# A decoder layer with 32 experts: contiguous rows in the gather, row splits between the transposes, gate loads on another queue

## The chip, the cores and the metric

The kernel runs on one core of a Trainium2 chip. A core has a matrix engine (TensorE, PE in the profile), a vector engine (VectorE, DVE), a scalar engine (ScalarE, ACT), GpSimd (POOL) and SyncE (SP), which here only issues transfers. Each engine works through its own list of instructions in order and waits on semaphores for the others. Sixteen DMA engines move data between the device memory and SBUF, the on-chip memory of 128 partitions; TensorE writes to PSUM, a small memory of banks of 512 float32 per partition.

The metric is the device time of one execution in microseconds (us). A profile is the record of one such execution.

## The reference

One layer on 256 tokens of 2048 features, all in float32. The mixers (a convolution, a gated linear attention, a windowed attention, a short convolution), the output projection and the first layer norm come first and are the same in both kernels. What the change touches comes after:

```python
x = layer_norm(DN_ALPHA * x + mix @ w_out[i], ln1_g[i], ln1_b[i])
ffn = hier_moe(x, ...)                       # 32 experts, two per token
ple = sigmoid(x @ ple_w_gate[i] + ple_b_gate[i]) * (p[i] @ ple_w_proj[i])
x = layer_norm(DN_ALPHA * x + ffn + ple, ln2_g[i], ln2_b[i])
```

In `hier_moe` each token picks one of four groups of experts by one softmax, then the two best of the eight experts in that group. An expert is `(silu(t @ w_gate) * (t @ w_up)) @ w_down` with 256 inner features, weighted by the router's gate. The weights of one expert are 6 MiB, so the 32 experts hold 192 MiB, and all but those of experts without tokens have to be read.

## The kernel before, in words

**Before the router.** The input projections, the mixers and the output projection take the first 408 us. Products run in a split form: a float32 matrix is cast to the faster format `fp32r` (high part), the rest is a second `fp32r` matrix (low part), and the products of the parts are added.

**The router stage** (L749 to L961). The rows are normalized without scale and bias (`xn`, tokens on the partitions). TensorE transposes them, two blocks of 128 features per step of the loop at L783, and the evictions from PSUM apply scale and bias, one block on DVE (L796), one on ACT (L793): that gives `x1T`, features on the partitions. The router's logits follow by matmuls (`route`). After the loop, `xn` is split for the gather: ACT casts four pieces of 1024 columns to `xnh` (L809), POOL subtracts four times to get `xnl` (L810). Then comes a chain of small DVE operations (L836 to L912): maxima, one-hot masks, counts, the order of the experts by their number of tokens, and a place (a "seat") for each token and expert. SP reads the order of the experts into registers before it issues the experts' weight loads.

**The gather** (L929). Ten groups have 128 seats each, in four units of 32; a unit belongs to one expert. `selection` builds a 0/1 matrix `M` (tokens by seats of two groups, 256 columns), and the gather is a matmul of rows of `xnh` and `xnl` with `M`, four per block of 128 features: 64 for all 16 blocks. Feature d = 16 p + k goes to partition p of block k, because the experts' weights lie in the device memory with 16 rows of a matrix behind each other on one partition; the 128 columns of `xn` that form the stationary operand of one matmul are therefore 16 elements apart (`k0 + j::KT`). The evictions apply scale and bias (`g16`, `b16`) on DVE and ACT. The first gather serves groups 0 and 1: half of it ahead of group 0, the rest between its first steps. The odd groups 1, 3, 5 and 7 carry the next gather between their own steps.

**The groups** (`experts`, L1027). For each group: `gu` matmuls of the gathered rows with gate and up weights in steps (8 steps when the group has four experts, 4 when it has two), each step reading one of five 2 MiB slots of SBUF; then silu and product on ACT and DVE, a transposition (`hT`), the down product in four steps of 512 columns (`y`), each followed by a scatter of the previous step (`sc`, the transposed selection matrix), which DVE adds into the result rows. Groups 0, 1, 2, 4, 8, 9 have four experts, groups 3, 5, 6, 7 two. In group 9 the loads of experts without tokens are skipped.

**The gate.** `ple` needs x1 @ ple_w_gate, a matmul of 256 x 2048 x 2048. It is cut into pieces (`layer_input_gate`, L720): for four column blocks db, 16 pieces of one feature block each, two token halves per piece; the end of a column block adds the product with `ple_w_proj`. The pieces fill TensorE between the steps of the groups: `pump(rate)` is called after each `gu` step, and `fill` after the silu, after `hT` and after each `y` step, which in the odd groups first takes the steps of the gather. `RT[g]` (L1143) says how many pieces a call gives. Eight short tasks that start the sum come before the pieces (`start_sum`), eight that spread the rows of the last norm behind. Two pieces and then one are issued in the router stage. Gate weights come in loads of 0.5 MiB for two pieces, into six buffers; the weights of pieces 9 to 32 (`in_slots`, pairs 4 to 15) lie instead in three of the five expert slots, which come free after pieces 16, 24 and 32.

**What sets the order.** TensorE's instructions in the groups, and those of TensorE, DVE and ACT in the router stage, stay in the order in which they are written; the other engines are ordered by a planner. SP issues all weight loads, those of the experts and of the gate, in one order, and waits at each for its buffer to be free.

Of the kernel before, what the change touches and what calls it, by code (L numbers as in the profile page):

```python
# [19 lines left out]
P = 128  # L20
# [69 lines left out]
def _layout(inp):  # L90

    lasting, early = _shape_tables()
    by_k = lambda w: w.reshape(KT, P, -1).transpose(1, 0, 2).reshape(P, -1)
    vec = lambda a: np.asarray(a).reshape(-1, P).T
    gla = Columns()
    for name in ("conf_dw_w", "conf_dw_b"):
        early.add(name, vec(inp[name]))
    for name in ("conf_ln_g", "conf_ln_b", "mix_scale", "gla_b_g2", "gla_norm_g",
                 "sc_conv_w", "ln1_g", "ln1_b"):
        lasting.add(name, vec(inp[name]))  # L100
    lasting.add("g16", np.asarray(inp["ln1_g"]).reshape(P, KT))
    lasting.add("b16", np.asarray(inp["ln1_b"]).reshape(P, KT))
    lasting.add("rbias", np.tile(np.concatenate([inp["router_g_b"][0], inp["router_e_b"][0]]), (P, 1)))
    vecs = np.zeros((2, 32, 512), np.float32)
    vecs[:, :20] = np.concatenate([np.asarray(inp[n]).reshape(4, 512) for n in
                                   ("ple_b_gate", "ln1_g", "ln1_b", "ln2_g", "ln2_b")])
    lasting.add("wr", by_k(np.concatenate([inp["router_g_w"][0], inp["router_e_w"][0]], axis=1)))
    w_in = np.asarray(inp["w_in"])[0]
    gla.add("wgl", by_k(np.pad(w_in[:, 2048:2064], ((0, 0), (0, 16)))))
    gla.add("wg2", np.tile(np.pad(inp["gla_w_g2"][0], ((0, 16), (0, 0))), (4, 1)))  # L110
    gla.add("relb", inp["rel_bias"])
    tiles = lambda w: w.reshape(2, 8, P, 512).transpose(0, 2, 1, 3)
    by_cols = lambda w: np.stack([tiles(w[:, c:c + 512]) for c in range(0, D, 512)])
    return {
        "vecs": vecs.reshape(64, 512), "lasting": lasting.array(), "early": early.array(), "gla": gla.array(),
        "xT": np.asarray(inp["x"])[0].T.reshape(KT, P, T).transpose(1, 0, 2),
        "x": inp["x"], "pT": np.asarray(inp["p"])[0, 0].T.reshape(2, P, T).transpose(1, 0, 2),
        "w_in": np.stack([tiles(w_in[:, c:c + 512]) for c in BLOCKS.values()]),
        "w_out": by_cols(np.asarray(inp["w_out"])[0]), "ple_w_gate": by_cols(np.asarray(inp["ple_w_gate"])[0]),
        "exp_w_gu": np.concatenate([inp["exp_w_gate"][0], inp["exp_w_up"][0]], axis=2),  # L120
        "exp_w_down": np.asarray(inp["exp_w_down"])[0], "ple_w_proj": np.asarray(inp["ple_w_proj"])[0],
    }, (lasting.at, early.at, gla.at)

# [2 lines left out]
def trunk(ctx, tc, where, vecs_d, lasting, early, gla, xT, x, pT_d, w_in, w_out, ple_w_gate, exp_w_gu, exp_w_down, ple_w_proj, out):  # L126
# [28 lines left out]
    def f32(ap):  # L155
        return ap.bitcast(F32)
# [544 lines left out]
    small = [(db, i) for db in range(4) for i in (*range(8 * db, 8 * db + 8), 32 + db) if i not in in_slots]  # L701
    ple_w = {}

    def ple_load(n=1):
        for _ in range(min(n, len(small))):
            db, i = small.pop(0)
            w = work([P, 2, 512], name="plw")
            if i < 32:
                nc.sync.dma_start(w, ple_w_gate[db, (i // 4) % 2, :, 2 * (i % 4):2 * (i % 4) + 2])
            else:  # L710
                nc.sync.dma_start(w, ple_w_proj[:, db * 512:(db + 1) * 512].rearrange("(k p) c -> p k c", p=P))
            ple_w[i] = w


# [32 lines left out]
    tasks.append(layer_input_gate())  # L747

    x1T = bm.tile([P, KT, T], F32, name="x1T", tag="ma")  # L749
    ple_load(6)  # L750
    for i in in_slots[::4]:
        s = load_half(ple_w_gate[i // 8, (i // 4) % 2], "plw")
        for j in range(4):
# [23 lines left out]
    def route(k2):  # L777
        for k in (2 * k2, 2 * k2 + 1):
            o = 64 * (k % 2)
            PE.matmul(rl[o:o + 36, 0:T], wr[:, k, :], x1T[:, k, :], start=k < 2, stop=k >= KT - 2,  # L780
                      skip_group_check=True, tile_position=(0, o))

    for k2 in range(KT // 2):  # L783
        b = bank("x1t", *tags[k2])
        for j in range(2):
            for t in range(NT):
                k = 2 * k2 + j
                PE.transpose(b[:, (j * NT + t) * P:(j * NT + t + 1) * P],
                             xs[t][k // 8][:, (k % 8) * P:(k % 8 + 1) * P], ident)
        for j in range(2):  # L790
            k = 2 * k2 + j
            if j:
                S.activation(x1T[:, k, :], b[:, j * T:(j + 1) * T], AF.Identity, scale=col("ln1_g", k),  # L793
                             bias=col("ln1_b", k))
            else:
                V.tensor_scalar(x1T[:, k, :], b[:, j * T:(j + 1) * T], col("ln1_g", k), col("ln1_b", k),  # L796
                                op0=ALU.mult, op1=ALU.add)
        if k2 > 2:
            route(k2 - 3)
    for k2 in range(KT // 2 - 3, KT // 2):  # L800
        route(k2)
    lt = stage([P, P], F32, name="lt", tag="mt", bufs=1)
    V.tensor_scalar(lt, const("io")[:, 0:P], const("sid")[:, 0:1], None, op0=ALU.is_gt)
    V.tensor_copy(rls[0:36, :], rl[0:36, 0:T])
    S.copy(rls[64:100, :], rl[64:100, 0:T])
    for hf in range(2):
        for t in range(NT):
            hs = slice(1024 * hf, 1024 * hf + 1024)
            S.copy(xnh[:, t, hs], xn[:, t, hs])  # L809
            G.tensor_sub(xnl[:, t, hs], xn[:, t, hs], f32(xnh[:, t, hs]))  # L810
    rl2 = bank("rl2")
    for t in range(NT):
        PE.matmul(rl2[:, 64 * t:64 * t + 36], rls[:, t * P:(t + 1) * P], both, start=t == 0, stop=True,
# [115 lines left out]
    def gather(m_, n, xg, tags=(("mx", 2),)):  # L929

        w = n * P
        per = 512 // w
        for k0 in range(0, KT, per):
            b = bank("xg", *tags[k0 // per % len(tags)])
            for j in range(per):
                o = b[:, j * w:(j + 1) * w]
                for t in range(NT):
                    for i, part in enumerate((xnh, xnl)):
                        PE.matmul(o, part[:, t, k0 + j::KT], m_[:, t, :], start=j + t + i == 0, stop=t + i == 2,  # L939
                                  skip_group_check=True)  # L940
            for j in range(per):
                k = k0 + j
                if j % 2:
                    S.activation(xg[:, k], b[:, j * w:(j + 1) * w], AF.Identity, scale=const("g16")[:, k:k + 1],  # L944
                                 bias=const("b16")[:, k:k + 1])
                else:
                    V.tensor_scalar(xg[:, k], b[:, j * w:(j + 1) * w], const("g16")[:, k:k + 1],  # L947
                                    const("b16")[:, k:k + 1], op0=ALU.mult, op1=ALU.add)
            yield

    def gathered(n):
# [75 lines left out]
    def experts(g, units, xg, xo, rate=0, last=False, ahead=None):  # L1027
# [20 lines left out]
        for k0 in range(0, KT, kn):  # L1048
            s = expert_slot("we", g)[:, 0:ne * kn * 512].rearrange("p (q k f) -> p q k f", q=ne, k=kn)
            for q in range(ne):  # L1050
                if k0 == 0:
                    es_.append(nc.sync.value_load(orders[0:1, ranks[q]:ranks[q] + 1], min_val=0, max_val=NE - 1))
                src = exp_w_gu[bass.ds(es_[q], 1)].rearrange("o (p k) f -> p (o k) f", p=P)
                nc.sync.dma_start(s[:, q], src[:, k0:k0 + kn, :], **need[q])

            if g == 0 and k0:
# [83 lines left out]
            pass  # L1140
        return xg

    RT = [1.6, 1.3, 2, 1.3, 0.6, 1, 0.6, 1.6]  # L1143
    RT += [0.5] * (NG - len(RT))
    tasks.insert(0, start_sum())
    tasks.append(second_norm_rows())
# [68 lines left out]
```

## Time and profile before

| | us |
|---|---|
| median of 3 runs | 1011.82 |
| lowest, highest | 1008.22, 1013.42 |
| profiled execution | 1012.47 |
| its span, first to last instruction | 1010.7 |
| first expert load issued by SP | 438.81 |
| first `gu` matmul of group 0 | 450.91 |
| last matmul | 988.66 |

A row of the time order gives the start, the length, the engine, the line, what is written and read, and the number of instructions merged in the row. Matmuls overlap: the length of one includes its way through the array, so what one costs is read from the start of the next. A row of the groups gives busy time and the mean of one in ns, then the idle time ahead of it and who ended it. A wait is put down to the engine that came last.

### The profile page before, as it was taken

The numbers are of one execution on the slowest core, as the hardware profiler recorded it, in microseconds if no ns is written. First come the engines' busy times: TensorE is split into PE (matmuls) and PEld (weight loads), VectorE is DVE, ScalarE is ACT, GpSimd is POOL, SyncE is SP. The second block draws the span as 40 slices with busy tenths as digits, with TensorE's granted clock in tenths as the row PEclk, the third lists the DMA queues.
The fourth block names the chain that finished last, engine by engine and source line by source line (L and its number), as shares of the span: only waits on it lengthen the run. The fifth ranks groups of instructions, "written<-read, shape, count | busy, mean of one in ns | idle before, by whom it ended". The sixth has DMA issues, their size and how long they took to land. (4 is left out here: it accounts for less than half of the span.)

```text
span 1010.7 us, 14886 instructions
## 1 busy us (share of the span) xinstructions
PE 937.8 (93%) x5542; PEld 580.7 (57%) x5542; DVE 454.1 (45%) x891; ACT 294.2 (29%) x529; POOL 147.9 (15%) x107
## 2 busy tenths in 40 slices
PE   8999998999999999869999999999998899998991
PEld 6896997978898789544333453333541263461220
DVE  6554648997758545665031141111431233340327
ACT  6631643444665445611010120100221021020002
POOL 2131335335323332310000000000000000000002
PEclk9999999999999999979999999999999999999996
DMA  9961364445345852048999999999489999989982
GB/s 336 418 235 73 124 222 135 164 161 183 152 163 193 323 201 85 19 171 335 363 327 409 395 404 408 391 415 342 170 309 388 417 418 368 411 330 398 362 312 86
DMA packets 76655, 280.90 MB, mean 278 GB/s; under 512 B 7000, under 2 KB 7264, under 8 KB 64544
## 3 DMA queue, kind: packets, MB, share of 16 engines
q1 hardware_dynamic: 76256, 278.82, 72.7%
q0 software_dynamic: 320, 1.06, 0.3%
q8 instruction: 45, 0.74, 0.3%
q14 instruction: 34, 0.28, 0.1%
HBM read 290.33 MB, written 2.11 MB: 289 GB/s over the span
## 5 line engine op out<-in xcount | busy, mean ns | idle before, releaser
L1060 PE MATMUL gu<-we,xg 128*32 128x512 f32 x1184 | 158.7, 600 | 7.8 <-DMA we<-in_exp_w_gu_dram 7.7
L730 PE MATMUL pl<-plw,x1T 128*128 128x512 f32 x256 | 120.9, 611 | 1.2 <-DMA plw<-in_ple_w_gate_dram 1.2
L1060 PEld LDWEIGHTS gu<-we,xg 128*32 128x32 f32 x1184 | 37.6, 110 | 111.6 <-issue 78.7
L1098 PE MATMUL y<-wd,hT 128*32 128x512 f32 x624 | 93.0, 599 | 8.3 <-DMA wd<-in_exp_w_down_dram 4.8
L1114 DVE TENSOR_TENSOR xn<-xn,sc 128x512 f32<-128x512 f32 x76 | 50.3, 683 | 106.3 <-PE sc L1112 106.3
L1180 POOL TENSOR_TENSOR xn<-xn,gbB 128x512 f32<-128x512 f32 x2 | 3.2, 1582 | 564.0 <-ACT xn L1179 564.0
L730 PEld LDWEIGHTS pl<-plw,x1T 128*128 128x128 f32 x256 | 46.7, 192 | 66.0 <-issue 62.7
L1080 DVE SCALAR_TENSOR_TENSOR h<-h,gw,gu 128x256 f32<-128x256 f32 x10 | 4.8, 480 | 173.9 <-ACT h L1079 173.9
L1079 ACT ACTIVATE h<-gu 128x256 f32<-128x256 f32 x10 | 3.8, 383 | 215.0 <-PE gu L1060 215.0
L939 PE MATMUL xg<-M,xnh 128*128 128x256 f32 x160 | 62.9, 393 | 2.7 <-DVE M L926 2.4
L483 DVE SCALAR_TENSOR_TENSOR ya<-hp,ce,ya 128x255 f32<-128x255 f32 (+29 forms) x120 | 63.9, 586 | 0.0
L939 PE MATMUL xg<-M,xnl 128*128 128x256 f32 x160 | 62.2, 389 | 0.0
L1102 ACT CAST yh<-y 128x512 fp32r<-128x512 f32 x40 | 23.4, 586 | 118.8 <-PE sc L1111 69.7
L939 PEld LDWEIGHTS xg<-M,xnh 128*128 128x128 f32 x160 | 50.1, 313 | 12.4 <-issue 4.5
L245 ACT CAST wh<-wow 128x512 fp32r<-128x512 f32 (+1 forms) x80 | 42.5, 535 | 44.4 <-PE wo L288 32.8
L1098 PEld LDWEIGHTS y<-wd,hT 128*32 128x32 f32 x624 | 19.2, 109 | 62.2 <-issue 28.8
L288 PE MATMUL wo<-wh,ml 128*128 128x512 f32 (+1 forms) x160 | 54.6, 350 | 0.0
L287 PE MATMUL wo<-wh,mh 128*128 128x512 f32 (+1 forms) x160 | 54.1, 348 | 0.0
L939 PEld LDWEIGHTS xg<-M,xnl 128*128 128x128 f32 x160 | 50.5, 315 | 0.1
L248 DVE TENSOR_TENSOR wl<-wow,wh 128x512 fp32r<-128x512 f32 (+1 forms) x53 | 31.8, 602 | 38.7 <-ACT wh L245 34.3
L1103 DVE TENSOR_TENSOR yl<-y,yh 128x512 fp32r<-128x512 f32 x40 | 27.4, 685 | 46.7 <-ACT yh L1102 46.1
L944 ACT ACTIVATE xg<-xg,cl 128x256 f32<-128x256 f32 x40 | 22.6, 564 | 85.2 <-DVE xg L947 85.2
(480 smaller groups left out, 1977.3 us busy)
## 6 DMA issues: line engine op xcount, KB each, us to landing
we<-in_exp_w_gu_dram SPq DMA_DIRECT2D x168, 512.0 KB, 7.4
wd<-in_exp_w_down_dram SPq DMA_DIRECT2D x92, 512.0 KB, 10.7
we<-in_exp_w_gu_dram SPq DMA_DIRECT2D x32, 1024.0 KB, 12.4
wow<-in_w_out_dram SPq DMA_DIRECT2D x16, 1024.0 KB, 7.2
wd<-in_exp_w_down_dram SPq DMA_DIRECT2D x16, 1024.0 KB, 10.2
wd<-in_exp_w_gu_dram SPq DMA_DIRECT2D x24, 512.0 KB, 5.5
plw<-in_ple_w_gate_dram SPq DMA_DIRECT2D x20, 512.0 KB, 10.3
plw<-in_ple_w_gate_dram SPq DMA_DIRECT2D x6, 1024.0 KB, 6.9
```

Source lines behind the costliest of these rows:

```text
L245: S.copy(wh, w)
L248: e.tensor_sub(wl, w, f32(wh))
L287: PE.matmul(o, lh[:, k, ts], wh, start=i == 0, stop=False)
L288: PE.matmul(o, ll(k)[:, ts], wh, start=False, stop=False)
L483: V.scalar_tensor_tensor(ya[:, cb, d:T], hp[:, cb, 0:T - d], dww(30 - d, cb), ya[:, cb, d:T], op0=ALU.mult, op1=ALU.add)
L730: PE.matmul(bs[t], x1T[:, k, t * P:(t + 1) * P], s, start=False, stop=k == KT - 1, skip_group_check=True)
L939: PE.matmul(o, part[:, t, k0 + j::KT], m_[:, t, :], start=j + t + i == 0, stop=t + i == 2, skip_group_check=True)
L1060: PE.matmul(gu[us, :], xg[:, k0 + k, xo + us.start:xo + us.stop], s[:, q, k, :], start=k0 + k == 0, stop=k0 + k == KT - 1, skip_group_chec ...
L1098: PE.matmul(y[us, :], hT[:, k, us], s[:, q, k, c0:c0 + 512], start=k == 0, stop=k == 1, skip_group_check=True, tile_position=(0, us.start))
L1102: S.copy(yh, y)
L1103: V.tensor_sub(yl, y, f32(yh))
L1114: V.tensor_add(rows(acc, t, db), rows(acc, t, db), o)
```

## The change

Five things change.

- The experts' gate and up weights are laid out so that feature d = 128 k + p is on partition p of block k. The gather reads 128 neighbouring columns of `xnh` and `xnl` for each matmul, and its evictions use the columns of scale and bias that the transposes use. `g16` and `b16` go.
- The split of `xn` moves from behind the transposes to between them: in step k2 ACT casts one piece of 512 columns, and DVE (no longer POOL) subtracts the piece of the step before. Eight casts and eight subtractions instead of four and four.
- The gate's loads, but for the first six, are issued by GpSimd instead of SP.
- `RT` changes: fewer gate pieces in groups 0 and 2, more in group 1, none in group 3, the last ones in group 4.
- The view of `exp_w_gu` in the load follows the new layout.

```diff
@@ _layout
-    lasting.add("g16", np.asarray(inp["ln1_g"]).reshape(P, KT))
-    lasting.add("b16", np.asarray(inp["ln1_b"]).reshape(P, KT))
...
-        "exp_w_gu": np.concatenate([inp["exp_w_gate"][0], inp["exp_w_up"][0]], axis=2),
+        "exp_w_gu": np.concatenate([inp["exp_w_gate"][0], inp["exp_w_up"][0]], axis=2)
+        .reshape(NE, KT, P, 2 * DE).transpose(0, 2, 1, 3),
@@ ple_load
-    def ple_load(n=1):
+    def ple_load(n=1, queue=G):
...
-                nc.sync.dma_start(w, ple_w_gate[db, (i // 4) % 2, :, 2 * (i % 4):2 * (i % 4) + 2])
+                queue.dma_start(w, ple_w_gate[db, (i // 4) % 2, :, 2 * (i % 4):2 * (i % 4) + 2])
...
-                nc.sync.dma_start(w, ple_w_proj[:, db * 512:(db + 1) * 512].rearrange("(k p) c -> p k c", p=P))
+                queue.dma_start(w, ple_w_proj[:, db * 512:(db + 1) * 512].rearrange("(k p) c -> p k c", p=P))
...
-    ple_load(6)
+    ple_load(6, nc.sync)
@@ router stage
+    def split_rows(i, low):
+
+        t, cs = i % 2, slice(512 * (i // 2), 512 * (i // 2) + 512)
+        if low:
+            V.tensor_sub(xnl[:, t, cs], xn[:, t, cs], f32(xnh[:, t, cs]))
+        else:
+            S.copy(xnh[:, t, cs], xn[:, t, cs])
+
     for k2 in range(KT // 2):
...
+        split_rows(k2, False)
+        if k2:
+            split_rows(k2 - 1, True)
         if k2 > 2:
             route(k2 - 3)
+    split_rows(7, True)
...
-    for hf in range(2):
-        for t in range(NT):
-            hs = slice(1024 * hf, 1024 * hf + 1024)
-            S.copy(xnh[:, t, hs], xn[:, t, hs])
-            G.tensor_sub(xnl[:, t, hs], xn[:, t, hs], f32(xnh[:, t, hs]))
@@ gather
-                        PE.matmul(o, part[:, t, k0 + j::KT], m_[:, t, :], start=j + t + i == 0, stop=t + i == 2,
+                        PE.matmul(o, part[:, t, (k0 + j) * P:(k0 + j + 1) * P], m_[:, t, :], start=j + t + i == 0, stop=t + i == 2,
                                   skip_group_check=True)
...
-                    S.activation(xg[:, k], b[:, j * w:(j + 1) * w], AF.Identity, scale=const("g16")[:, k:k + 1],
-                                 bias=const("b16")[:, k:k + 1])
+                    S.activation(xg[:, k], b[:, j * w:(j + 1) * w], AF.Identity, scale=col("ln1_g", k),
+                                 bias=col("ln1_b", k))
                 else:
-                    V.tensor_scalar(xg[:, k], b[:, j * w:(j + 1) * w], const("g16")[:, k:k + 1],
-                                    const("b16")[:, k:k + 1], op0=ALU.mult, op1=ALU.add)
+                    V.tensor_scalar(xg[:, k], b[:, j * w:(j + 1) * w], col("ln1_g", k), col("ln1_b", k), op0=ALU.mult, op1=ALU.add)
@@ experts
-                src = exp_w_gu[bass.ds(es_[q], 1)].rearrange("o (p k) f -> p (o k) f", p=P)
+                src = exp_w_gu[bass.ds(es_[q], 1)].rearrange("o p k f -> p (o k) f")
@@ rates of the filler
-    RT = [1.6, 1.3, 2, 1.3, 0.6, 1, 0.6, 1.6]
+    RT = [1.3, 2.5, 1.3, 0, 1]
     RT += [0.5] * (NG - len(RT))
```

## The prediction

> **What bounds the kernel now.** I read the page first, then the work by stretches of time, then single instructions in order of time. From the page come the busy shares and the DMA row (the span in 40 slices, each digit tenths of the 16 DMA engines).
>
> ```profile
> PE 937.8 (93%) x5542; PEld 580.7 (57%) x5542; DVE 454.1 (45%) x891; ACT 294.2 (29%) x529; POOL 147.9 (15%) x107
> DMA  9961364445345852048999999999489999989982
> ```
>
> TensorE looks full everywhere; the DMA engines are slack early, idle around slice 17, then full, with holes. So the expert part (from about 440 us) has two near-limits, and the router ahead of it is a chain of small steps. Next, the expert part by stretches: the first gather, then the ten groups, each cut where its first `gu` matmul starts. Columns: stretch, us, busy PE, PEld, DVE, ACT, POOL (counts), granted clock, DMA share, GB/s.
>
> ```profile
> 438.81:450.91 12.10, 12.02 (x39) 8.94 (x38) 6.52 (x28) 2.00 (x5) 0.00 (x0) 0.81 0.88 307
> 450.91:534.80 83.89, 80.52 (x325) 31.44 (x324) 26.59 (x47) 12.02 (x18) 0.00 (x0) 0.98 0.92 336
> 534.80:596.75 61.95, 61.66 (x315) 29.96 (x314) 13.53 (x25) 6.95 (x13) 0.00 (x0) 1.00 1.03 401
> 596.75:686.92 90.17, 88.93 (x351) 33.46 (x350) 16.25 (x28) 11.18 (x15) 0.00 (x0) 1.00 1.03 405
> 686.92:743.02 56.10, 53.75 (x304) 28.28 (x303) 16.91 (x31) 9.32 (x16) 0.00 (x0) 0.97 0.66 241
> 743.02:790.28 47.26, 43.01 (x219) 11.32 (x218) 9.82 (x20) 9.53 (x16) 0.00 (x0) 1.00 1.01 383
> 790.28:836.18 45.90, 42.81 (x276) 24.19 (x275) 14.99 (x27) 6.96 (x13) 0.00 (x0) 1.00 1.01 416
> 836.18:864.86 28.68, 26.51 (x212) 8.74 (x211) 9.84 (x20) 3.66 (x7) 0.00 (x0) 1.00 0.98 375
> 864.86:905.41 40.55, 40.55 (x276) 23.27 (x275) 14.98 (x27) 6.96 (x13) 0.00 (x0) 1.00 0.95 373
> 905.41:951.74 46.33, 40.79 (x212) 10.29 (x211) 10.04 (x23) 3.66 (x7) 0.00 (x0) 1.00 1.02 383
> 951.74:989.06 37.32, 34.84 (x223) 11.49 (x222) 12.34 (x21) 4.61 (x9) 0.00 (x0) 1.00 0.80 282
> ```
>
> Length times GB/s gives the bytes: 198.1 MB. The five groups at a DMA share of 1.01 or more (1, 2, 4, 5, 8) move 116.3 MB in 291.6 us: 399 GB/s is a full stream here, and 198.1 MB take 496 us at it. SP's first expert load, and the 5 us stretch in which the stream ends (0.30 of it busy, so at 982.5):
>
> ```profile
> 438.81 29.15 SPq L1054 DMA_DIRECT2D we<-in_exp_w_gu_dram  x20
> 981.00:986.00 5.00, 4.69 (x36) 1.63 (x34) 4.51 (x8) 0.59 (x1) 0.00 (x0) 1.00 0.30 111
> ```
>
> The stream lasts 543.7 us, so 47 us are idle: 16 up to the end of group 0 (31.9 MB need 80 of 96 us), 22 in group 3 (13.5 MB need 34 of 56), 4 in groups 6 and 7, 4 in group 9. Group 3 is where TensorE lags: it comes out of group 2 (90 us, stuffed with gate pieces) with all five weight slots full, so SP cannot load; then groups 4 and 8 wait for weights.
>
> **The router stage.** DVE and POOL rows in order of time (start, length):
>
> ```profile
> 420.93 0.42 DVE L804 COPY rls<-rl 36x256 f32<-36x256 f32 x1 [1.22 <-PE rl L780]
> 422.95 9.26 POOL L810 TENSOR_TENSOR xnl<-xn,xnh 128x1024 fp32r<-128x1024 f32 x4 [17.17 <-ACT xnh L809]
> 423.00 2.34 DVE L843 TENSOR_TENSOR rt<-rt 128x8 f32<-128x8 f32 x1
> 429.97 2.32 DVE L851 TENSOR_TENSOR rt<-rt 128x64 f32<-128x64 f32 x1
> 432.33 0.27 DVE L853 TENSOR_REDUCE rt<-rt 128x16 f32<-128x64 f32 x1
> 432.83 0.18 DVE L843 TENSOR_TENSOR rt<-rt 128x16 f32<-128x16 f32 x1
> ```
>
> While POOL subtracts (four of 2.3 us, to 432.2), an 8-element operation of DVE takes 2.3 us; the same line takes 0.18 us afterwards. Five operations fill 423.00 to 432.33; at 0.21 each they need 1.05. These run on the path that releases the expert loads, so taking the subtractions off POOL gives **8.3 us**. The Trainium skill, page "SBUF — State Buffer", section "Who interferes with whom", says that a DVE instruction with two SBUF inputs and a GpSimd instruction that reads SBUF exclude each other for the whole instruction; the rows agree, each stall being one POOL operation long. Were the cause instead ACT's casts at that time, the 8.3 would stay and the sum be 8.3 higher.
>
> The price is paid between the transposes: eight casts more on ACT there, eight 512-wide subtractions on DVE. Rows: the first four DVE evictions, and a DVE subtraction of the same form.
>
> ```profile
> 413.08 1.90 DVE L796 TENSOR_SCALAR x1T<-x1t,cl 128x256 f32<-128x256 f32 x4 [0.64 <-PE x1t L788]
> L1103 DVE TENSOR_TENSOR yl<-y,yh 128x512 fp32r<-128x512 f32 x40 | 27.4, 685 | 46.7 <-ACT yh L1102 46.1
> ```
>
> DVE becomes the loop's limit: 8 x (0.475 + 0.68) = 9.2 us from 413.08, to 422.3 instead of 420.93: **+1.4**. Below, nothing (hidden); above, DVE eviction, ACT eviction and ACT cast one after the other, 8 x (0.5 + 0.56 + 0.6) = 13.3, or +5.5. I take 1.4, because a subtraction is placed a step behind its cast. Net −6.9: the stream starts at 431.9.
>
> **The gather.** Starts of successive matmuls show what one costs: first the gather now, then a projection of the same form (256 columns, fp32r, 128x128 weights) whose rows are contiguous.
>
> ```profile
> 449.04 0.39 PE L939 MATMUL xg<-M,xnh 128*128 128x256 f32 x1
> 449.26 0.39 PE L939 MATMUL xg<-M,xnl 128*128 128x256 f32 x1
> 402.79 0.28 PE L288 MATMUL wo<-wh,ml 128*128 128x256 f32 x1
> 402.91 0.28 PE L287 MATMUL wo<-wh,mh 128*128 128x256 f32 x1
> ```
>
> 0.22 against 0.12 us: with 64 matmuls a gather falls from 14.2 to 7.5 us of TensorE. Bounds: 0.222 (no gain) and 0.117; the form is the same, so I take 0.117. The moved layout of the expert weights keeps the bytes and the run per partition of each load: 0. The columns for scale and bias are only renamed: 0.
>
> **Pieces of TensorE work**, each from its start to the next one's (expert step, gate piece, gate's end, row spread; then a down step with its scatter):
>
> ```profile
> 603.18 1.92 PE L1060 MATMUL gu<-we,xg 128*32 128x512 f32 x16
> 605.04 1.98 PE L730 MATMUL pl<-plw,x1T 128*128 128x512 f32 x4
> 606.86 3.60 PE L741 MATMUL pr<-plw,pT 128*128 128x512 f32 x8
> 610.38 0.73 PE L717 MATMUL pl<-vecs,pick 64*128 64x512 f32 x2
> 611.04 1.99 PE L730 MATMUL pl<-plw,x1T 128*128 128x512 f32 x4
> 585.65 1.93 PE L1098 MATMUL y<-wd,hT 128*32 128x512 f32 x16
> 587.50 0.50 PE L1111 MATMUL sc<-yh,MT 128*128 128x512 f32 x1
> 588.54 0.28 PE L939 MATMUL xg<-M,xnh 128*128 128x256 f32 x1
> ```
>
> An expert step costs 1.86, a gate piece 1.82, a gate's end 4.2, a down step with scatter 2.9. A group's core is 8 x 1.86 + 4 x 2.9 + 0.3 = 26.7. Calls of the filler (one per `gu` step, and seven more where no gather takes them) times its rate give the gate pieces: before 16, 10, 30, 5 in groups 0 to 3 (15 x 1.6 less 8 sums; 8 x 1.3; 15 x 2; 4 x 1.3). It checks: group 2 is 26.7 + 30 x 1.82 + 2 x 4.2 = 89.7, measured 90.2. After: 15 x 1.3 less 8 is 11; 8 x 2.5 is 20; 20; none; 10 in group 4.
>
> TensorE's own time after: group 0, 26.7 + 3.7 (second half of the gather) + 6.6 (sums, broadcasts) + 20 = 57; group 1, 26.7 + 8 + 36.4 + 8.4 = 79.5; group 2, 67; group 3, 34.7; group 4, 51; then 35, 29, 35, 27 and 37. Loading at 399 GB/s: 63 for four experts, 31.5 for two (24 and 12 MiB), 1.3 per gate load. Group 0's stream cannot end before 431.9 + 2 + 67 + 8 = 509, and TensorE then stands at 590, 657 and 692 after groups 1, 2 and 3 (each the sum so far), while their loads, two and nine gate loads among them, are done at 575, 650 and 682: a lead of 7 to 15 us, under the 25 that five slots hold, so nothing forces the stream to stop. After group 4 the loads (749) are the later one; up to group 7 the two stay within 10 us, and group 8 waits for its loads again. So TensorE's saved time is worth what it frees in the stream: idle falls from 47 to 8 + 2 + 1 + 4.4 = 15.4. Group 0 keeps half of its 16, since three of five slots still hold gate weights until pieces 16, 24 and 32 (bounds 2 and 16); group 3 keeps 2 of 22 (bounds 0 and 11); group 9's 4.4 stay. **−31.5.**
>
> **The queue.** 18 loads of gate weights leave SP for POOL:
>
> ```profile
> SPq L709 <- PE pl L730: 47.2, 5, 45.2
> L531 POOL DMA_DIRECT2D trev<-gdram x2: 748/779/810, 168.2 to 169.0; - x2
> DMA to landing us min/median/max: 5.3/10.3/12.8
> ```
>
> SP waited 47.2 us for a gate buffer, 45.2 in one wait before the router, when no expert load could go; 2 us remain. POOL pays some 0.78 us per issue, with nothing else until the last normalization. Behind SP's wait stood expert loads; behind POOL's stands nothing. I take 0 (bounds −2 and, if POOL's 18 x 0.78 stalled DVE, 14 us on an engine 18 to 32% busy there: hidden). The Trainium skill speaks against this part: page "DMA: Bandwidth & Descriptors", section "Issuing engines are not separate DMA queues", says that another issuing engine saves only issue time; by it the sum is the same.
>
> **Sum.** 1012.47 (the profiled execution; the median is 1011.82) − 6.9 − 31.5 = **974 us**.
>
> **Rivals.** *The pitch stays* at 0.22 for another reason than the rows' stride. Then 3.4 us stay ahead of group 0 and 6.7 in groups 1, 3, 5 and 7; the lead passes 25 us in groups 3 and 7, and some 9 us of idle come back: about 986. For it: weight load and matmul overlap, so their lengths alone don't prove it. *The gate starves the ring in group 1*: 79.5 us of TensorE against 66 of loading, and if the held slots come free late, the stream loses those 13.5: 988. *Transfers hidden anyway*: the stream keeps its 47 idle, only the router and half a gather's 3.4 remain: 1002. Against it: 22 of the 47 lie in one place, whose cause moves. *The other side: late gate loads.* A gate piece stands in TensorE's fixed order ahead of expert steps. Six buffers of two pieces give a load five buffers, or 10 pieces, of cover: four steps of 6.4 us, 25 us. Landing took at most 12.8. If POOL's queue landed them after 28 us, 18 waits of 3 us (54) would eat the 38.4 and end at about 1028; it decides from 27 us on, where 18 x 2.1 is the 38.4.
>
> **Chances.** Forecast 0.60, pitch 0.08, starved ring 0.15, hidden transfers 0.06, late loads 0.06, and 0.05 that nothing measurable happens, gains and losses cancelling. A difference of 0.5% is about what can be told from none. All cases but the last two are faster by more: 0.89; same 0.05, slower 0.06. The range: low, all idle but 4 gone and the casts hidden (1012.47 − 8.3 − 43 = 961), and the stream at 405 GB/s as in group 2, 7 less: 954; high, the starved ring (988) with the cast chain (+4.1) and group 3 keeping 9 more: 1001. I take 953 to 1000; hidden transfers, no change and late loads lie outside.
>
> **What would show it.** Right: no DVE operation above 0.5 us in the router chain; gather matmuls 0.12 us apart; group 3 under 38 us at a DMA share near 1; first expert load near 432. Wrong: group 1 above 85 us with DMA share below 0.9; TensorE waiting on gate loads; a gather held by its evictions.

## The result, and the profile after

| | before | after |
|---|---|---|
| median, us | 1010.56 (4 runs, 1008.22 to 1013.42) | 973.36 (4 runs, 971.69 to 974.50) |
| profiled execution, its span | 1012.47, 1010.7 | 974.50, 972.7 |
| first expert load issued | 438.81 | 432.98 |
| first `gu` matmul of group 0 | 450.91 | 443.16 |
| last matmul | 988.66 | 951.16 |

The ratio is 0.9629, with a 95% interval of 0.9598 to 0.9660. The forecast was 974. In the experiments below, one execution with two slots lent and one with the queue alone took 4798 us, and one of the kernel before 1451 us; the ratios and intervals leave these three out.

In the new kernel's code the lines move: the transposes' eviction on DVE is L803, the split's cast and subtraction L788 and L786, a gate piece L729, the gather L945, the `gu` step L1065, the `y` step L1103, the loads of the experts' first and second weights L1059 and L1097, a gate load L708.

First the page of the new kernel: busy shares, and the DMA engines in 40 slices.

```profile
PE 909.9 (94%) x5542; PEld 547.3 (56%) x5542; DVE 448.1 (46%) x899; ACT 292.1 (30%) x531; POOL 148.6 (15%) x121
DMA  9961454544343784028999999999999999999972
```

The same number of TensorE instructions is 27.9 us shorter, and the DMA row has no hole left between slice 19 and the tail. Where the span went shows in the expert part, cut at the same events as before (columns as before: stretch, us, busy PE, PEld, DVE, ACT, POOL, granted clock, DMA share, GB/s):

```profile
432.98:443.16 10.18, 8.09 (x39) 6.37 (x39) 6.52 (x28) 1.69 (x5) 0.00 (x0) 0.83 0.91 321
443.16:519.03 75.87, 70.99 (x295) 23.66 (x294) 23.11 (x41) 9.97 (x16) 1.60 (x3) 1.00 0.95 345
519.03:598.60 79.57, 79.52 (x376) 34.46 (x375) 19.04 (x35) 10.07 (x17) 1.59 (x3) 1.00 1.01 386
598.60:666.49 67.89, 67.89 (x301) 24.37 (x300) 14.11 (x27) 7.88 (x12) 5.50 (x10) 1.00 1.03 406
666.49:704.38 37.89, 35.66 (x275) 16.83 (x274) 13.08 (x25) 6.41 (x12) 0.72 (x1) 1.00 1.02 412
704.38:758.86 54.48, 54.10 (x264) 17.89 (x264) 13.14 (x26) 8.92 (x15) 0.00 (x0) 1.00 1.03 401
758.86:798.72 39.86, 37.91 (x278) 17.95 (x277) 14.10 (x26) 9.45 (x16) 0.00 (x0) 1.00 1.02 416
...
911.95:951.55 39.60, 36.05 (x223) 11.25 (x222) 12.31 (x21) 4.59 (x9) 0.00 (x0) 1.00 0.77 273
941.00:946.00 5.00, 3.77 (x20) 1.03 (x19) 3.06 (x5) 0.59 (x1) 0.00 (x0) 1.00 0.58 209
```

Group 3, where the stream stood still for 22 us, now has a share of 1.02. The last row puts the end of the stream at 941 + 0.58 x 5 = 943.9, so it lasts 510.9 us instead of 543.7. The span's change adds up from three pieces: the stream starts 5.8 earlier, is 32.8 shorter, and what follows it is 0.6 longer (28.8 against 28.2): −38.0, from 1010.7 to 972.7.

The first piece is the router. The new kernel's DVE rows there, in order of time: the loop's first three and last three, three operations of the chain, the chain's last, and the counts.

```profile
412.11 0.99 DVE L803 TENSOR_SCALAR x1T<-x1t,cl 128x256 f32<-128x256 f32 x2 [0.64 <-PE x1t L795]
413.79 0.69 DVE L786 TENSOR_TENSOR xnl<-xn,xnh 128x512 fp32r<-128x512 f32 x1 [0.69 <-ACT xnh L788]
414.40 0.54 DVE L803 TENSOR_SCALAR x1T<-x1t,cl 128x256 f32<-128x256 f32 x1
...
420.65 0.69 DVE L786 TENSOR_TENSOR xnl<-xn,xnh 128x512 fp32r<-128x512 f32 x1
421.70 0.69 DVE L786 TENSOR_TENSOR xnl<-xn,xnh 128x512 fp32r<-128x512 f32 x1 [0.36 <-ACT xnh L788]
...
422.50 0.41 DVE L815 COPY rls<-rl 36x256 f32<-36x256 f32 x1
424.56 0.17 DVE L849 TENSOR_TENSOR rt<-rt 128x8 f32<-128x8 f32 x1
425.37 0.23 DVE L857 TENSOR_TENSOR rt<-rt 128x64 f32<-128x64 f32 x1
...
428.48 0.22 DVE L869 TENSOR_TENSOR rt<-rt 128x64 f32<-128x64 f32 x1
430.43 0.18 DVE L877 SCALAR_TENSOR_TENSOR rt<-cn,cl 32x32 f32<-32x32 f32 x1 [1.73 <-PE cn L875]
```

The two operations that took 2.34 and 2.32 us now take 0.17 and 0.23. The loop ends later: the copy of the logits starts 10.39 us after the first eviction, against 7.85 before (420.93 less 413.08). And the counts wait 1.73 us for TensorE, where the kernel before had waited 0.74; the forecast has no such wait. TensorE's rows and its granted clock at that place:

```profile
423.46 0.60 PE L819 MATMUL rl<-both,rls 128*128 128x36 f32 x4 [1.62 <-ACT rls L816]
...
424.66 5.40 PE L729 MATMUL pl<-plw,x1T 128*128 128x512 f32 x8
429.99 0.31 PE L873 MATMUL cn<-rt,ones 128*32 128x32 f32 x4
```

```profile
424.00:426.00 2.00, 2.00 (x5) 0.92 (x5) 1.62 (x9) 1.97 (x3) 0.00 (x0) 0.73 0.00 0
426.00:428.00 2.00, 2.00 (x4) 0.68 (x3) 1.66 (x10) 0.34 (x2) 0.00 (x0) 0.50 0.00 0
```

The two gate pieces that fill the router take 5.40 us, and the granted clock falls to 0.5 under them. In the kernel before, the same eight matmuls took 3.70, and the counts waited less:

```profile
423.09 3.70 PE L730 MATMUL pl<-plw,x1T 128*128 128x512 f32 x8
436.15 0.18 DVE L871 SCALAR_TENSOR_TENSOR rt<-cn,cl 32x32 f32<-32x32 f32 x1 [0.74 <-PE cn L869]
```

The pieces were once hidden under a chain that the stalls had stretched to 12.9 us. With the chain at 4.6 us, pieces of 5.4 us are no longer covered.

### The profile page after: what moved, and what is told of

Its sections match the earlier page's. It is cut to its first block, busy times and chain, and to the rows that moved or that the text cites. A ratio compares the mean times of both kernels' runs of the same rounds, so it can differ in the third digit from the quotient of the medians.

```text
span 972.7 us, 14900 instructions
## 1 busy us (share of the span) xinstructions
PE 909.9 (94%) x5542; PEld 547.3 (56%) x5542; DVE 448.1 (46%) x899; ACT 292.1 (30%) x531; POOL 148.6 (15%) x121
## 5 line engine op out<-in xcount | busy, mean ns | idle before, releaser
L1065 PE MATMUL gu<-we,xg 128*32 128x512 f32 x1184 | 166.0, 597 | 9.0 <-DMA we<-in_exp_w_gu_dram 9.0
L729 PE MATMUL pl<-plw,x1T 128*128 128x512 f32 x256 | 120.8, 611 | 0.0
L1065 PEld LDWEIGHTS gu<-we,xg 128*32 128x32 f32 x1184 | 38.1, 109 | 119.2 <-issue 72.1
L1103 PE MATMUL y<-wd,hT 128*32 128x512 f32 x624 | 86.7, 608 | 5.8 <-DMA wd<-in_exp_w_down_dram 2.5
L729 PEld LDWEIGHTS pl<-plw,x1T 128*128 128x128 f32 x256 | 46.7, 192 | 64.8 <-issue 63.8
L287 PE MATMUL wo<-wh,ml 128*128 128x512 f32 (+1 forms) x160 | 54.5, 350 | 0.0
L1103 PEld LDWEIGHTS y<-wd,hT 128*32 128x32 f32 x624 | 18.6, 110 | 53.1 <-issue 28.7
L708 POOL DMA_DIRECT2D plw<-in_ple_w_gate_dram x16 | 8.5, 534 | 241.9 <-PE pl L729 157.9
L945 PE MATMUL xg<-M,xnh 128*128 128x256 f32 x160 | 42.6, 301 | 2.5 <-DVE M L932 2.1
L288 PE MATMUL wo<-wl,mh 128*128 128x512 f32 (+1 forms) x160 | 43.8, 351 | 0.1
L247 POOL TENSOR_TENSOR wl<-wow,wh 128x512 fp32r<-128x512 f32 (+1 forms) x27 | 30.7, 1139 | 68.8 <-ACT wh L244 54.5
## 6 DMA issues: line engine op xcount, KB each, us to landing
wd<-in_exp_w_down_dram SPq DMA_DIRECT2D x92, 512.0 KB, 10.4
```

The costliest lines, as they stand in the source:

```text
L247: e.tensor_sub(wl, w, f32(wh))
L287: PE.matmul(o, ll(k)[:, ts], wh, start=False, stop=False)
L288: PE.matmul(o, lh[:, k, ts], wl, start=False, stop=i == KT - 1)
L729: PE.matmul(bs[t], x1T[:, k, t * P:(t + 1) * P], s, start=False, stop=k == KT - 1, skip_group_check=True)
L945: PE.matmul(o, part[:, t, (k0 + j) * P:(k0 + j + 1) * P], m_[:, t, :], start=j + t + i == 0, stop=t + i == 2, skip_group_check=True)
L1065: PE.matmul(gu[us, :], xg[:, k0 + k, xo + us.start:xo + us.stop], s[:, q, k, :], start=k0 + k == 0, stop=k0 + k == KT - 1, skip_group_chec ...
```

## The experiments

### One part put back

Four kernels are the new one with one of its parts as before. Each expectation gives what the part should be worth.

The old rates of the filler:

```diff
-    RT = [1.3, 2.5, 1.3, 0, 1]
+    RT = [1.6, 1.3, 2, 1.3, 0.6, 1, 0.6, 1.6]
```

> The kernel after, with the filler's rates of before (16, 10, 30 and 5 gate pieces in groups 0 to 3). Theory (the stream of loads is the bound, and TensorE matters only where it holds the slots): group 2 is long again (90 us), group 3 has gate pieces, so the five slots fill and the stream idles some 12 us in and behind group 3: 985 us, against 973 of the kernel after. Rival 1 (the contiguous gather alone frees the stream, the rates add nothing): 973. Rival 2 (the rates are the whole gain, the gather is hidden): 1000 or more.

989.44 us (ratio 0.9790, interval 0.9763 to 0.9818), 16.1 above the new kernel and 4 more than expected. Groups 2 and 3 of this kernel:

```profile
587.01:676.01 89.00, 89.00 (x351) 33.79 (x351) 16.37 (x29) 11.72 (x16) 7.31 (x13) 1.00 1.03 409
676.01:725.91 49.90, 47.50 (x303) 21.64 (x303) 16.45 (x31) 8.78 (x15) 0.00 (x0) 1.00 0.75 289
```

The hole is back, behind a group of 89 us: 14.4 MB (49.90 x 289) need 36.1 us at 399 GB/s, so 13.8 are idle. With the contiguous gather it is smaller than the 22 of before, since group 3 itself is shorter.

The gather's rows 16 elements apart, with the old layout of the weights and `g16`, `b16`:

```diff
-    part[:, t, (k0 + j) * P:(k0 + j + 1) * P], m_[:, t, :]
+    part[:, t, k0 + j::KT], m_[:, t, :]
```

> The kernel after, with the experts' weights and the gather's rows as before (16 elements apart). Theory: gather matmuls stand 0.22 us apart again; 6.7 us come back in groups 1, 3, 5 and 7 each, some 24 us of TensorE up to the end of group 7, of which the lead of the loads takes up 9: 986 to 988. Rival 1 (transfers hidden anyway): under 977. Rival 2 (pitch not from the rows' stride): pitch stays 0.12 us in the trace, 973.

985.83 us (0.9758, 0.9727 to 0.9789), 12.5 above, as expected. First two matmuls of the gather in group 1 of this kernel, and then two in group 1 of the new kernel; what one costs is read from start to start:

```profile
592.00 0.39 PE L946 MATMUL xg<-M,xnh 128*128 128x256 f32 x1
592.22 0.39 PE L946 MATMUL xg<-M,xnl 128*128 128x256 f32 x1
```

```profile
588.97 0.28 PE L945 MATMUL xg<-M,xnh 128*128 128x256 f32 x1
589.09 0.28 PE L945 MATMUL xg<-M,xnl 128*128 128x256 f32 x1
```

0.22 against 0.12 us, with nothing changed but the stride of the columns of the stationary operand (and the feature order that goes with it). The odd groups 1, 3, 5 and 7 grow from 79.6, 37.9, 39.9 and 34.5 to 85.3, 41.1, 41.8 and 40.5 us, and the stream falls short again in the groups that follow: shares of 0.97 and 0.94 in groups 6 and 7.

The split back behind the transposes and on POOL:

> The kernel after, with the split of the rows behind the transposes and the subtractions on POOL, as before. Theory (POOL's subtractions stop DVE's two-input operations in the router chain): first expert load 5 us later against the end of the output projection, DVE operations of 2.3 us in the chain, 978. Rival (the stream makes up for a late start, or the casts between the transposes cost what the lock did): 973.

977.85 us (0.9679, 0.9653 to 0.9704), 4.5 above, as expected; the first expert load goes out at 437.08 instead of 432.98, and every group after the first gather has its length to within 1.8 us. What the split's place is worth is the time at which the stream starts.

The gate loads back on SP:

```diff
-                queue.dma_start(w, ple_w_gate[...])
+                nc.sync.dma_start(w, ple_w_gate[...])
```

> The kernel after, with all gate loads on SP's queue. Theory: the queue is worth nothing, 972 to 975. Rival 1 (SP's waits for a gate buffer hold up the expert loads behind them, now that the gate pieces are packed into group 1): 978 or more, with SP waits at the gate loads and a lower DMA share in groups 1 and 2. Rival 2 (loads issued by POOL disturb the others): under 970.

977.62 us (0.9663, 0.9638 to 0.9689), 4.3 above by the medians and 3.4 by the ratios. That is the rival's case and not the theory's, though in group 0, where the rival looked for it in groups 1 and 2. The intervals of this kernel and of the new one overlap at their edges, so the size is loose; the place is plain. Both reach group 0 at the same time (443.18 and 443.16). Group 0 of this kernel, SP's rows inside it, and TensorE's wait for down weights over the whole execution (us in total, times, longest):

```profile
443.18:524.86 81.68, 72.72 (x296) 23.76 (x295) 23.11 (x41) 9.99 (x16) 0.00 (x0) 0.98 0.91 327
```

```profile
485.72 0.68 SPq L708 DMA_DIRECT2D plw<-in_ple_w_gate_dram  x1
488.65 4.08 SPq L1097 DMA_DIRECT2D wd<-in_exp_w_down_dram  x4
492.83 3.22 SPq L708 DMA_DIRECT2D plw<-in_ple_w_gate_dram  x2
499.55 7.17 SPq L1097 DMA_DIRECT2D wd<-in_exp_w_down_dram  x7
```

```profile
PE y L1103 <- DMA wd<-in_exp_w_down_dram: 6.1, 8, 2.8
```

In the new kernel:

```profile
480.96 24.18 SPq L1097 DMA_DIRECT2D wd<-in_exp_w_down_dram  x15
```

```profile
PE y L1103 <- DMA wd<-in_exp_w_down_dram: 2.5, 7, 0.7
```

SP works through its list in order. A gate load has to wait until TensorE has used up the piece before it, and the loads of down weights stand behind it; TensorE then waits for these. With the gate loads elsewhere SP issues 15 loads without a gate load between them, and group 0 is 5.8 us shorter. Inside group 0 TensorE waits 7.8 us for expert weights here (4.3 for down weights, 3.5 for gate and up weights) and 3.7 in the new kernel (1.0 and 2.7): that is 4.1 of the 5.8. The rest lies in matmuls that are longer on average (72.72 us busy against 70.99, at a granted clock of 0.98 against 1.00). The Trainium skill, page "DMA: Bandwidth & Descriptors", section "Issuing engines are not separate DMA queues", says that issuing from several engines saves only the sequencer's time to issue. The measurement differs here, and it decides: what was saved is the time that other loads wait in line behind a load that isn't allowed to go yet.

### One part alone

The same four parts, each put into the kernel before by itself.

> The kernel before with only the filler's new rates. Theory: the idle of the stream in group 3 goes, but the slow gathers hold groups 1, 3, 5 and 7: about 991 us against 1010.6 of before. Rival (gather and rates act on the same idle time, each alone gives nearly all of it): 980. Rival 2 (with the slow gather, group 1 at 86 us starves the ring): 1005 or more.

> The kernel before with only the contiguous gather and its layout. Theory: 6.7 us less in groups 1 and 3, 3.4 each ahead of and in group 0, so the stream idles some 20 us less: about 989. Rival (hidden, since the loads bind anyway): 1007.

> The kernel before with only the split between the transposes on ACT and DVE. Theory: the stream starts 5 us earlier and nothing behind it changes: 1005 to 1006. Rival (groups 2 and 3 hold the ring whatever its start): 1010.

> The kernel before with only the gate loads on POOL's queue. Theory: 1009 to 1011.5, no difference. Rival (SP waits for gate buffers in group 2 while expert loads could go): 1005 or less.

| part | alone, us | ratio (interval) | gain alone | loss when put back |
|---|---|---|---|---|
| rates | 992.41 | 0.9812 (0.9781 to 0.9843) | 18.3 | 16.1 |
| gather | 995.04 | 0.9845 (0.9822 to 0.9868) | 15.7 | 12.5 |
| split | 1005.13 | 0.9950 (0.9934 to 0.9967) | 5.6 | 4.5 |
| queue | 1009.23 | 0.9982 (0.9968 to 0.9997) | 1.5 | 4.3 |

The gains alone (against 1010.7, the median of the kernel before beside them) sum to 41.1, the losses to 37.4, and all together gave 37.2. Taken from the ratios, each of which has the kernel before beside it, the losses are 16.3, 13.0, 5.1 and 3.4. Rates, split and queue came out within 1.5 us of what was expected. So the parts are nearly independent. Rates and gather seem to overlap a little; both take TensorE's work out of the groups around the hole, but the two were not run together without the rest. The gather alone fell 6 us short of its expectation; its groups 2 and 3:

```profile
591.69:685.09 93.40, 91.38 (x352) 33.87 (x351) 16.38 (x29) 11.72 (x16) 0.00 (x0) 0.98 1.03 409
685.09:735.00 49.91, 47.51 (x304) 21.66 (x303) 16.46 (x31) 8.76 (x15) 0.00 (x0) 1.00 0.72 254
```

The faster gather makes group 3 6.2 us shorter, but group 2 was here 3.2 us longer than before (at a granted clock of 0.98; the runs don't show why), and the hole stays: 254 GB/s in 49.91 us leaves 18 us idle. The queue seems to be worth more with the other parts (3.4 to 4.3) than without (1.5), though the first number is loose. A reason fits the rows: before, group 0 is set by TensorE's 16 gate pieces and the gather (83.67 us with the queue moved, 83.89 without), so loads that come earlier have nothing to shorten.

### Fewer slots lent to the gate

The forecast left 8 us idle in group 0, because three of the five expert slots hold gate weights when the experts' loads begin. With two slots lent instead of three, one more slot is free from the start, and eight gate pieces more go through the small buffers:

```diff
-    NPRE = 3
+    NPRE = 2
```

> The kernel after with two instead of three expert slots filled with gate weights ahead of the router, so three slots are free for the experts in group 0; four gate loads (2.1 MB, 5.2 us at 399 GB/s) move from the idle time before the router into the stream. Theory (group 0's 12 us of idle stream come from the two slots left): idle up to the end of group 0 falls from 12 to some 5 us, the stream carries 5.2 us more, 971 to 973. Rival (the idle comes from something else, the late first steps or the chain behind the last gu step): idle stays 12, and the time is 978.

965.92 us (0.9557, 0.9528 to 0.9587). That is 7.4 below the new kernel, and better than the 971 to 973 expected. Groups 0 and 1:

```profile
444.25:511.92 67.67, 65.16 (x296) 22.99 (x295) 23.12 (x41) 9.98 (x16) 1.79 (x3) 1.00 1.03 400
511.92:591.09 79.17, 79.12 (x375) 34.34 (x375) 19.04 (x35) 10.07 (x17) 3.74 (x7) 1.00 1.03 404
```

Both run at a full stream, 400 and 404 GB/s where the new kernel has 345 and 386. The held slots are the cause of the idle that was left in the first two groups; the expectation had missed that group 1 gains as well.

### The clock in the router

If the wait of 1.73 us comes from a throttled clock, short matmuls into an unused bank during TensorE's waits should remove it. 17 of them were put in at three places, in addition to the kernel's work:

```diff
+            PE.matmul(aw[:, 0:P], ones, ones, start=True, stop=True)
```

> The kernel after with 17 matmuls of 128 columns, whose result nobody reads, in TensorE's waits of the router stage (6 ahead of the logits' sum, 3 and 8 around the counts). Theory (TensorE's waits there lower the granted clock to 0.5, which makes the two gate pieces take 5.4 instead of 3.7 us on the path and keeps the first gather at 0.21 us a matmul): clock 1.00 from 424 to 444, the first gather 3.9 us, group 0 some 3 us earlier, 970 to 971. Rival (the stream of loads decides, group 0's start does not matter): clock 1.00, but 973.

973.61 us (0.9637, 0.9611 to 0.9663): no change that the medians show, where 970 to 971 was expected. The two gate pieces of this kernel, its granted clock over the router, and the clock in a stretch behind it:

```profile
425.38 3.70 PE L729 MATMUL pl<-plw,x1T 128*128 128x512 f32 x8
```

```profile
418.00:432.00 14.00, 13.28 (x72) 7.08 (x70) 10.46 (x43) 9.01 (x15) 0.56 (x1) 1.00 0.10 25
434.00:436.00 2.00, 2.00 (x4) 0.96 (x3) 1.82 (x11) 0.30 (x2) 0.00 (x0) 0.50 0.84 303
```

The clock stays at 1.00 where it had fallen to 0.5, and the two gate pieces take 3.70 us again, so the cause of the longer pieces is shown. But the clock then falls one step later, in the third gate piece, against the expectation. The first gather does run in the 3.9 us that were expected, with its matmuls 0.12 us apart, but the eight added matmuls ahead of it delay its start. Counted from the first eviction (412.84 here, 412.11 in the new kernel) the first load goes out 1.2 us earlier and group 0 starts 1.9 us earlier. So the wait is worth about a microsecond at its place. Counted the same way, group 9 starts 1.5 us earlier (911.22 less 412.84 against 911.95 less 412.11), and so does the end of the span. So in these two executions the stream did not swallow the gain, as it should have by the rival; but 1.5 us is less than the medians can tell from nothing, and the rival is neither shown nor refuted.

### The split's price

Does DVE have to pay for the subtractions? Here POOL does them, at the same place between the transposes:

```diff
-            V.tensor_sub(xnl[:, t, cs], xn[:, t, cs], f32(xnh[:, t, cs]))
+            G.tensor_sub(xnl[:, t, cs], xn[:, t, cs], f32(xnh[:, t, cs]))
```

> The kernel after with the eight subtractions between the transposes on POOL instead of DVE. Theory (only DVE operations with two inputs in SBUF wait for POOL): the evictions on DVE, with one input from PSUM, keep 0.54 us; the loop falls back to 1.15 us a step, the logits are copied 1.5 to 2.5 us earlier, and only the last subtraction can touch the chain: 971 to 972. Rival (any DVE operation waits for POOL): evictions of 1 us and more, the loop longer, 976 or more.

968.90 us (0.9600, 0.9565 to 0.9635), 4.5 below the new kernel by the medians (1.5 to 2.5 were expected) and 2.9 by the ratios. Its ratio lies just inside the new kernel's interval (0.9598 to 0.9660), so the gain in the whole is not clear of noise; what happens in the router is. POOL's and then DVE's rows of this kernel:

```profile
413.84 9.88 POOL L786 TENSOR_TENSOR xnl<-xn,xnh 128x512 fp32r<-128x512 f32 x8 [9.02 <-ACT xnh L788]
```

```profile
414.57 0.55 DVE L803 TENSOR_SCALAR x1T<-x1t,cl 128x256 f32<-128x256 f32 x1 [0.56 <-PE x1t L795]
420.85 0.42 DVE L815 COPY rls<-rl 36x256 f32<-36x256 f32 x1 [1.95 <-PE rl L779]
422.73 0.16 DVE L848 TENSOR_REDUCE rt<-rt 128x2 f32<-128x8 f32 x1
422.92 0.82 DVE L849 TENSOR_TENSOR rt<-rt 128x8 f32<-128x8 f32 x1
```

POOL subtracts from 413.84 to 423.72. All that time the evictions, whose input lies in PSUM, keep their 0.54 to 0.55 us: POOL holds none of them. Nor does it hold the reduction with one input in SBUF (L848, 0.16). It holds the chain's first operation with both inputs in SBUF: 0.82 us instead of 0.17, until the last subtraction is over. One other operation of that time is longer than in the new kernel, the 128x128 one at L814 with one input (0.43 against 0.28); the rows don't say why. ACT's last cast had ended by 420.58. The copy of the logits starts 8.74 us after the first eviction, 1.65 earlier than in the new kernel. The Trainium skill, page "SBUF — State Buffer", section "Who interferes with whom", says that a vector instruction with at most one input in SBUF doesn't contend with GpSimd (outside some fast modes), and one with two does; the evictions, the reduction and L849 agree with it, and whether L814 falls under the modes it excepts no run here shows. So the stall of the kernel before came from the moment of the subtractions, not from POOL as such.

### Both together

Two slots lent, and the subtractions between the transposes on POOL:

> The changed kernel with two alterations that were each timed alone: two instead of three expert slots lent to the gate weights (965.92, 7.4 below the changed kernel's 973.36), and the eight subtractions between the transposes on POOL instead of DVE (968.9, 4.5 below). If the one frees the stream of weights inside group 0 and the other lets the same stream start 2 us earlier, the gains add: about 961.5, first expert load near 431, group 0 at about 400 GB/s. Rival: TensorE's own work in groups 0 and 1 is what now limits, so that an earlier start of the stream buys less: about 964 to 966.

965.33 us (0.9533, 0.9512 to 0.9553). This is the lowest median of all and beats the new kernel by 8.0, but it can't be told from two slots lent alone. The median lies in the rival's 964 to 966 and not at 961.5. Whether the gains add is not decided: by the medians they don't (7.4 and 4.5 alone, 8.0 together), by the ratios they nearly do (7.3 and 2.9 alone, 9.7 together). The first load goes out 432.31 − 413.11 = 19.2 us after the first eviction, 1.6 less than with two slots lent (434.06 − 413.26 = 20.8). The groups:

```profile
442.49:510.07 67.58, 64.99 (x295) 22.78 (x294) 23.12 (x41) 9.66 (x15) 1.79 (x3) 1.00 1.03 397
510.07:589.25 79.18, 79.13 (x376) 34.35 (x375) 19.05 (x35) 10.08 (x17) 3.74 (x7) 1.00 1.03 405
```

From the first load to the start of group 9 both kernels take 471.6 us, so up to there the earlier start of the stream is kept whole; the rival's reason, that TensorE in groups 0 and 1 takes it back, does not show. Of the 1.6 us the last group and the tail gave back about 1. With three slots lent, the two profiled executions differ by 5.1 us: 2.2 is the earlier first load, 0.9 lies between it and group 9 (478.06 against 478.97), and 2.2 in group 9, which takes 37.43 us with POOL subtracting and 39.60 in the new kernel. Nothing in group 9 was altered, and it took 37.84 and 39.39 in other variants of the new kernel, so these 2.2 can't be credited to POOL's subtractions.

## Why the prediction was right, point by point

**Lock in the router: right.** Forecast −8.3. The chain from its first operation to its last ahead of the counts took 12.86 us before and takes 4.60 (424.10 to 428.70): −8.26. That ACT's casts were the cause is out too. In the kernel before they end at 425.66, and two-input operations of 2.07 and 2.32 us follow up to 432.29. And with POOL subtracting between the transposes the chain's first two-input operation was still held, over 2 us after the last cast.

**Price of the split: mis-sized.** The step "DVE becomes the loop's limit: 8 x (0.475 + 0.68)" gave +1.4; measured +2.5 (10.39 less 7.85). The sum of DVE's work was right, 9.3 of the 10.4 us. What it left out is that DVE and ACT alternate: DVE waits 0.69 for the first cast and 0.36 for the last. The bounds of 0 to 5.5 held it.

**A wait that was missed.** The counts' wait for TensorE grew from 0.74 to 1.73. The step that took −8.3 as the whole answer didn't ask what is late next: the gate pieces under the chain, and at half clock. The router is worth −8.3 + 2.5 + 1.0 = −4.8 instead of −6.9; from the first eviction to the first load it took 25.73 us before and takes 20.87. The first load moved by −5.8, because this execution reached the router 1.0 us earlier; that is no part of the change.

**The gather: right on its price.** 0.12 us apart in the groups, as taken. The first gather is the exception: its matmuls run partly at a granted clock of 0.5, 0.21 us apart.

```profile
439.01 0.41 PE L945 MATMUL xg<-M,xnl 128*128 128x256 f32 x1
439.22 0.41 PE L945 MATMUL xg<-M,xnh 128*128 128x256 f32 x1
```

```profile
440.00:442.00 2.00, 2.00 (x12) 2.00 (x11) 0.54 (x1) 0.74 (x2) 0.00 (x0) 0.50 0.96 365
```

So the time from the first load to group 0 fell by 1.9 us (12.10 to 10.18) and not by 3.4. The rival that the pitch stays is out: the pitch fell, and in the run that puts the stride back it is 0.22 again. That run at the same time measured the rival's price: 985.8 where it said 986.

**The stream: right in sum, by errors that cancel.** Idle at 399 GB/s was to fall from 47 to 15.4; 510.9 us for 198.3 MB leave 14. Place by place: up to the end of group 0 it is 12.3, not 8; group 1 leaves 2.6, not 0; group 3 none, not 2; group 9 4.9, not 4.4. Against these 5 us too much stands that groups 2 to 7 load at 401 to 416 GB/s, faster than the 399 taken as full, worth 6.5. The 399 was a mean of groups between 383 and 416 in the kernel before, where group 5 already ran at 416, so it was too low for a full stream. The lengths of TensorE's groups held: 79.57 for 79.5, 67.9 for 67, but 37.9 for 34.7 and 54.5 for 51 in groups 3 and 4. The times at which the groups end did not: groups 1, 2 and 3 were to end at 590, 657 and 692 and end at 598.6, 666.5 and 704.4, because group 0 ends at 519.0 where the working has its stream end at 509. The total was added up from the idle times and did not use these times. That it met the median to within a microsecond is luck: its terms are off by up to 6 us, in both directions.

**The queue: mis-sized, and the reason named.** "I take 0 (bounds −2 and ...)": the run with the loads back on SP says −3.4 to −4.3, loosely, beyond the lower bound of −2. Since the sum took the queue at nothing, its 974 stands just as well for the kernel with the loads on SP, and that one took 977.6. The step judged SP by its waits in the kernel before, 2 us of gate waits behind the router. It should have asked for SP's waits under the new rates, where gate pieces stand closer to the loads of down weights. The idle up to the end of group 0 was to be halved although the slots stay held. What it did lose was bought by the queue: with the loads on SP, it is 17.5 (9.37 us at 282 GB/s and 81.68 at 327), with them on POOL 12.3, and with one slot fewer held 2.5.

**The other rivals.** Hidden transfers (1002) fell: the hole in group 3 did close. The starved ring in group 1 (988) fell: 386 GB/s instead of 399, 2.6 us. Late gate loads (1028) fell: TensorE's list of waits has none for a gate load from POOL's queue, which lands in 7.0 us, against the 27 from which it would decide:

```profile
plw<-in_ple_w_gate_dram POOLq DMA_DIRECT2D x16, 512.0 KB, 7.0
```

**The sum.** Router +2.1 against the forecast, the earlier start −1.0, the stream −1.3, the tail +0.6: +0.4 on the forecast for the profiled execution, 974.1 to 974.5.

## What to carry to other kernels

When a stream of loads is the floor, count its idle time place by place and ask of each place which engine holds the buffers; filler work moved from the group that lags to one that has slack was here worth about as much as a faster gather (18.3 and 15.7 us, each alone). A load that has to wait for its buffer belongs on a queue where nothing urgent stands behind it, and this has to be asked again after every change of the order. After a stall is removed, look at what it was hiding: here two gate pieces at half the granted clock came to light.

## What the runs showed of the hardware

- The granted TensorE clock fell to 0.5 in the router behind a wait of only 1.62 us that was followed by short matmuls (36 columns); where the wait at the same place was 1.10 (the kernel before) or 1.07 (POOL subtracting between the transposes), the two gate pieces behind it took 3.70 us instead of 5.40. Matmuls of 128 columns put into the waits kept it at 1.00 up to 432 us, and then it fell to 0.5 once more, in the third gate piece, behind a wait of 0.53. How much idle time brings the clock down was not separated from how short the matmuls around it are.
- At a granted clock of 0.5 a gather with contiguous columns costs 0.21 us per matmul, about what one with columns 16 elements apart costs at full clock, 0.22. The granted clock in the rows tells the two apart.
- A stream of expert loads ran at 401 to 416 GB/s over whole groups (2 to 7 of the new kernel), above the mean of 399 that the kernel before had shown over its five fullest.
